# A two-layer encoder trunk on one core: thirteen instead of ten of the second layer's channel-mix double units as seven half-size products, and a higher pace for the sums of weights

## The chip, the cores and the metric

The kernel runs on one NeuronCore of a Trainium2 chip. The metric is the device time of one execution in microseconds (us). A profiled execution adds a trace of every engine: TensorE (PE, with its weight loads shown apart as PEld), VectorE (DVE), ScalarE (ACT), GpSimd (POOL) and SyncE (SP), which here only issues transfers.

## What is computed

The reference is a trunk of two layers over 512 frames of 1024 channels, in float32. Each layer has an mLSTM branch, a retention branch, a merge, a channel mix and a per-layer embedding. The change touches the weights of the channel mix alone:

```python
h2 = rmsnorm(x, norm2_g[i])
x = x + jnp.square(jax.nn.relu(h2 @ w_ff1[i] + b_ff1[i])) @ w_ff2[i] + b_ff2[i]
```

`w_ff1` is 1024 x 4096 and `w_ff2` is 4096 x 1024. "The first product" is the one with `w_ff1`.

## The kernel before

**Units.** Activations lie transposed, channels on the 128 partitions and the 512 frames along a row. A float32 product is made of three matmuls on a value's rounded part (`h`) and its remainder (`l`): `h*h`, `l*h` and `h*l` (lines 480 to 482, 531 to 533 and 575 to 577 of the kernel). All work on TensorE is a list of units (`unit_list`), 275 of them, and the weights of each are loaded by SP, rounded by ScalarE (line 303, tiles `wh_...`) and reduced to their remainder by VectorE (line 304, tiles `wl_...`). Four raw buffers (`wr`) and three pairs of rounded ones stand ahead of TensorE.

**A plain unit (T8)** makes 128 output channels: 8 blocks of 128 input channels times 3 matmuls, each 128 x 128 by 512 frames, 24 matmuls. **A double unit** makes 256 output channels, either as two T8 (48 matmuls of 512 frames) or as a **PAIR**: seven products of half-size blocks in the manner of Strassen and Winograd, named P1 to P7, each of 4 blocks times 3 matmuls over 256 frames (84 matmuls of 256 frames). `run_pair` issues P1, P5, then what the unit before has left over (`flush`), then P6, P2, P3 and P7. Its own P4 is left over, and comes after P5 of the next unit. P1, P6, P7 and P4 follow each other in one PSUM bank (`a`), so P6 can't add to it before P1 has been copied out:

```python
def evict(x, o):
    if x == "P1":
        ac.activation(y[0][:, b], o, AF.Copy)
    elif x == "P5":
        ac.activation(y[1][:, a], o, AF.Copy)
...
        ve.tensor_tensor(y[0][:, b], o, y[0][:, b], OP.add)
```

P1, P5, P6 and P4 are copied out by ScalarE (lines 602, 604, 608 and 614), P2, P3 and P7 added by VectorE (606, 610 and 612).

**Weights of a PAIR.** Seven operands are needed: four given quarters of the weights, of which three are used as they are, and four sums of quarters (`t1` to `t4`). They come in four pieces: A, B and C of 128 x 1024 and D of 128 x 512. For a double unit of the second layer's first product all four sums are made ahead in DRAM, by transfers that add at their destination. GpSimd issues them (line 361, tiles `s...t`). `step` issues one, and `tick` counts a credit that lets the next one go: each unit adds `SHARE` (until the first layer's last gate unit) or `LATER` (after it) times the unit's time less its load, and each sum takes `STEP`. A sum's issue waits for the matmul that stands last at that point. A load of a summed operand waits for its sum.

**The channel mix.** `FPAIRS` names, for each layer, the double units (b, p) of the first product that are a PAIR, where b is one of four blocks of 1024 hidden channels and p one of four double units in it. They are called f02 for (0, 2) and so on below, with layer 1 in the trace's names (`l1f02a`: layer 1 counted from 0, PSUM bank a). The sixteen double units of the second product (o00 to o33) are all PAIRs. The order is f00 to f03, f10, o00 to o03, f11, f12, f13, f20, o10 to o13, f21, f22, f23, f30, o20 to o23, f31 to f33, o30 to o33.

**What follows a unit f (`ff1`).** Each has a tile `st` of 128 x 2048, which holds its 256 x 512 results (as four quarters) and four sums of them. There are two such tiles, taken in turn:

```python
st = cur["ff"].tile([P, 8 * S], F32, name=nm + "st", tag="st", bufs=2)
```

In a PAIR the evictions write into `st` at once, from P1 on. In a unit of two T8, `st` is first written when a T8 has ended. Then come, for each half d: the factor of the norm on VectorE (line 1485), relu and square on ScalarE (1486 and 1487). The second half of channels (d = 1) doesn't need P4, the first one does. Then `pair_quarters` rounds three quarters (`l1hh` by ScalarE, `l1hl` by VectorE, 128 x 768), and `pair_operand` makes four sums (lines 621, 622 and 623 on VectorE) and rounds these (128 x 1024). Only then is the tile `st` free for the unit after the next.

Each engine takes its instructions in one fixed order, which a scheduler writes when the program is built. It puts evictions ahead of what is not due yet.

Of the kernel before, what the change touches and what calls it, by code (L numbers as in the profile page):

```python
# [86 lines left out]

FPAIRS = (((1, 1), (1, 3), (2, 1), (2, 3), (3, 1)), ((0, 2), (1, 0), (1, 1), (1, 3), (2, 0), (2, 1), (2, 3), (3, 0), (3, 1), (3, 2)))  # L90


PRODUCTS = {"P1": ("A", 0, 0), "P5": ("A", 1, 4), "P2": ("B", 0, 2), "P6": ("B", 1, 5), "P3": ("C", 0, 6),
# [14 lines left out]
HALVES = [(WIDE[x][0], u) for x, u in TURNS]  # L108

SOON = ("w_in", 0, CGM + 2 * P)  # L110
STEP, SHARE, LATER = 1.13, 0.75, 0.75
TIME = {"PAIR": (9.9, 3.9), "WIDE": (5.45, 2.7), "FULL": (9.9, 5.0)}


# [32 lines left out]
def groups():  # L147
# [3 lines left out]
    for i in range(L):  # L151
# [11 lines left out]
        for b in range(4):  # L163
            f = [p for c, p in FPAIRS[i] if c == b]
            if f:
# [5 lines left out]
def unit_list(i):  # L171
# [10 lines left out]
    def pair(g, p):  # L182
        u.append(("PAIR", (i, g), p))
# [51 lines left out]
    def pairs(seq):  # L235
        for kind, b, p in seq:
            if (b, p) in FPAIRS[i] and kind == "f":
                pair(f"fp{b}", [q for c, q in FPAIRS[i] if c == b].index(p))
            elif kind == "f":
# [13 lines left out]
def build(ctx, tc, ins, out):  # L253
# [721 lines left out]
    for i in range(L):  # L975
# [501 lines left out]
        def ff1(b, p):  # L1477
# [10 lines left out]

            if (b, p) in FPAIRS[i]:
                def consume(y):  # L1490
                    for d in range(2):
                        evac(d, y[d], SIGN[d])
                    pair_quarters(st, *hid[b, p])
                    pair_operand(nm, st, *hid[b, p])
# [306 lines left out]
```

## Time and profile before

| | |
|---|---|
| three runs | 2314.02, 2317.37 and 2317.66 us, median 2317.37 |
| the profiled execution's own time | 2315.14 us |
| its span, first to last instruction | 2313.4 us |
| PE busy | 2299.1 us (99%) |
| DVE busy | 1766.8 us (76%) |
| ACT busy | 1269.6 us (55%) |
| POOL busy | 624.1 us (27%) |
| granted TensorE clock, mean | 0.998 |
| moved by DMA | 499.36 MB, mean 216 GB/s |

The times of a trace count from the span's start. A row of the timeline has the start, the duration, the engine, the line, the operation, `out<-in`, and in brackets how long the engine had been idle and for whom. The records of two instructions that follow each other without a pause overlap somewhat, so the cost of one in a chain is the distance of two starts. The channel mix of the second layer lies between 1915 and 2250 us.

### The profile page before, as it was taken

The numbers are of one execution on the slowest core, as the hardware profiler recorded it, in microseconds if no ns is written. First come the engines' busy times: TensorE is split into PE (matmuls) and PEld (weight loads), VectorE is DVE, ScalarE is ACT, GpSimd is POOL, SyncE is SP. The second block draws the span as 40 slices with busy tenths as digits, with TensorE's granted clock in tenths as the row PEclk, the third lists the DMA queues.
The fourth block names the chain that finished last, engine by engine and source line by source line (L and its number), as shares of the span: only waits on it lengthen the run. The fifth ranks groups of instructions, "written<-read, shape, count | busy, mean of one in ns | idle before, by whom it ended". The sixth has DMA issues, their size and how long they took to land.

```text
span 2313.4 us, 36468 instructions
## 1 busy us (share of the span) xinstructions
PE 2299.1 (99%) x13532; PEld 2035.4 (88%) x13532; DVE 1766.8 (76%) x2690; ACT 1269.6 (55%) x1837; POOL 624.1 (27%) x984
## 2 busy tenths in 40 slices
PE   9999999999999999999999999999999999999998
PEld 8888899888898899999888888988888888999997
DVE  7878767886676878788778777778867678787785
ACT  6756544644554546556557564445445446566564
POOL 4333222223124322223442332221231242111112
PEclk9999999999999999999999999999999999999999
DMA  7776787777789888888886768877877898878851
GB/s 218 189 191 174 238 228 216 215 227 210 232 230 261 220 228 223 240 239 215 222 224 182 196 174 247 232 216 216 223 221 208 241 266 218 247 232 228 232 160 55
DMA packets 187603, 499.36 MB, mean 216 GB/s; under 512 B 26064, under 2 KB 29520, under 8 KB 187424
## 3 DMA queue, kind: packets, MB, share of 16 engines
q0 software_dynamic: 57520, 188.53, 37.1%
q1 hardware_dynamic: 114496, 281.06, 36.6%
q10 hardware_dynamic: 15408, 27.43, 3.5%
q8 instruction: 106, 1.74, 0.3%
q14 instruction: 73, 0.60, 0.1%
HBM read 478.05 MB, written 194.51 MB: 291 GB/s over the span
## 4 chain that ended last, share of the span: by engine, by line
PE 92%; DVE 5%; ACT 1%; issue 1%; DMA 1%; POOL 0%; SPq 0%; ACTq 0%; DVEq 0%; POOLq 0%
PE l0br L480 1%; PE l1br L480 1%; PE l1br L481 1%; PE l0br L482 1%; PE l1br L482 1%; PE l0br L481 1%; PE l0f L480 1%; PE l0f L481 1%; PE l0f L482 1%; PE l1f L480 1%; PE l1f L481 1%; PE l1f L482 1%; PE l0pg L480 1%; PE l1bm L480 1%; PE l0pg L482 1%
## 5 line engine op out<-in xcount | busy, mean ns | idle before, releaser
L303 ACT ACTIVATE wh<-wr 128x1024 fp32r<-128x1024 f32 (+1 forms) x193 | 199.7, 1041 | 140.5 <-issue 17.1
L304 DVE TENSOR_TENSOR wl<-wr,wh 128x1024 fp32r<-128x1024 f32 (+1 forms) x191 | 234.6, 1230 | 37.5 <-ACT wh L303 36.9
L303 ACT ACTIVATE wh_B<-wr 128x1024 fp32r<-128x1024 f32 x123 | 130.3, 1059 | 184.5 <-PE l0br L481 15.7
L304 DVE TENSOR_TENSOR wl_B<-wr,wh_B 128x1024 fp32r<-128x1024 f32 x123 | 150.3, 1222 | 55.1 <-ACT wh_B L303 50.6
L303 ACT ACTIVATE wh_C<-wr 128x1024 fp32r<-128x1024 f32 x75 | 79.2, 1056 | 69.5 <-PE l0br L481 8.3
L304 DVE TENSOR_TENSOR wl_C<-wr,wh_C 128x1024 fp32r<-128x1024 f32 x75 | 91.7, 1223 | 21.3 <-ACT wh_C L303 17.1
L303 ACT ACTIVATE wh_A<-wr 128x1024 fp32r<-128x1024 f32 x75 | 78.9, 1052 | 44.3 <-DMA wr<-wpairs 5.2
L304 DVE TENSOR_TENSOR wl_A<-wr,wh_A 128x1024 fp32r<-128x1024 f32 x75 | 91.6, 1221 | 12.6 <-ACT wh_A L303 9.4
L303 ACT ACTIVATE wh_D<-wr 128x512 fp32r<-128x512 f32 x75 | 47.2, 630 | 96.5 <-DVE wr L462 27.3
L303 ACT ACTIVATE wh_t<-wr 128x1024 fp32r<-128x1024 f32 x56 | 59.4, 1061 | 69.0 <-PE l0g2va L576 6.0
L304 DVE TENSOR_TENSOR wl_t<-wr,wh_t 128x1024 fp32r<-128x1024 f32 x56 | 68.2, 1221 | 26.1 <-ACT wh_t L303 25.5
L304 DVE TENSOR_TENSOR wl_D<-wr,wh_D 128x512 fp32r<-128x512 f32 x75 | 51.8, 690 | 30.2 <-ACT wh_D L303 28.7
L480 PE MATMUL l0f<-l0n2h,wh 128*128 128x512 f32 x176 | 68.7, 390 | 0.0
L481 PE MATMUL l0f<-l0n2l,wh 128*128 128x512 f32 x176 | 68.6, 390 | 0.0
L482 PE MATMUL l0f<-l0n2h,wl 128*128 128x512 f32 x176 | 68.5, 389 | 0.0
L361 POOL DMA_DIRECT2D s30t<-wpairs x24 | 16.8, 699 | 92.4 <-PE l1o11a L533 9.4
L482 PEld LDWEIGHTS l0f<-l0n2h,wl 128*128 128x128 f32 x176 | 33.0, 188 | 7.0
L480 PEld LDWEIGHTS l0f<-l0n2h,wh 128*128 128x128 f32 x176 | 33.1, 188 | 6.6
L481 PEld LDWEIGHTS l0f<-l0n2l,wh 128*128 128x128 f32 x176 | 33.1, 188 | 6.5
L480 PE MATMUL l1f<-l1n2h,wh 128*128 128x512 f32 x96 | 37.6, 391 | 0.0
L481 PE MATMUL l1f<-l1n2l,wh 128*128 128x512 f32 x96 | 37.5, 390 | 0.0
L482 PE MATMUL l1f<-l1n2h,wl 128*128 128x512 f32 x96 | 37.4, 389 | 0.0
(5797 smaller groups left out, 9132.4 us busy)
## 6 DMA issues: line engine op xcount, KB each, us to landing
wr<-wstream SPq DMA_DIRECT2D x189, 512.0 KB, 4.8
wr<-wpairs SPq DMA_DIRECT2D x225, 256.0 KB, 4.1
wr<-wwide SPq DMA_DIRECT2D x48, 512.0 KB, 4.7
s3t<-wwide POOLq DMA_DIRECT2D x24, 256.0 KB, 5.0
s6t<-wwide POOLq DMA_DIRECT2D x24, 256.0 KB, 5.0
s18t<-wwide POOLq DMA_DIRECT2D x24, 256.0 KB, 4.7
s21t<-wwide POOLq DMA_DIRECT2D x24, 256.0 KB, 5.3
s24t<-wpairs POOLq DMA_DIRECT2D x24, 256.0 KB, 5.7
```

The costliest lines, as they stand in the source:

```text
L303: a = ac.activation(hi_ap, src, AF.Copy)
L304: return a, ve.tensor_sub(lo_ap, src, hi_ap.bitcast(F32))
L361: dma = gp.dma_start(piece(g, x, p, q), piece(g, MADE[x][a], p, q), max_dma_last_dim=4096, **kw)
L480: te.matmul(o, sh, mh, start=first, stop=False)
L481: te.matmul(o, sh, ml, start=False, stop=False)
L482: cur["mm"] = te.matmul(o, sl, mh, start=False, stop=last)
```

## The change

Two constants change. The second layer's tuple of `FPAIRS` gains (0, 3), (1, 2) and (2, 2), and `LATER` goes from 0.75 to 0.79:

```diff
-FPAIRS = (((1, 1), (1, 3), (2, 1), (2, 3), (3, 1)), ((0, 2), (1, 0), (1, 1), (1, 3), (2, 0), (2, 1), (2, 3), (3, 0), (3, 1), (3, 2)))
+FPAIRS = (((1, 1), (1, 3), (2, 1), (2, 3), (3, 1)), ((0, 2), (0, 3), (1, 0), (1, 1), (1, 2), (1, 3), (2, 0), (2, 1), (2, 2), (2, 3), (3, 0), (3, 1), (3, 2)))
...
-STEP, SHARE, LATER = 1.13, 0.75, 0.75
+STEP, SHARE, LATER = 1.13, 0.75, 0.79
```

So f03, f12 and f22 become PAIRs: 6 T8 units go and 3 PAIRs come (272 units instead of 275). Sums of weights rise from 670 to 694 transfers, and the loads by SP by 15. The order of all engines around the three units is written anew. Three places matter.

**ScalarE, from f13's rest to f20's evictions.** Before, where f12 is two T8 (`wh_B`, `wh_D`, `wh_A` are the weights of this and the next unit):

```order
L608 ACTIVATE l1f13st<-l1f13a 128x256
L303 ACTIVATE wh_C<-wr_20741 128x1024
L303 ACTIVATE l1hh_20628<-l1f12st 128x1024
L303 ACTIVATE wh_B<-wr_20763 128x1024
L602 ACTIVATE l1f20st<-l1f20a 128x256
L604 ACTIVATE l1f20st<-l1f20c 128x256
L1486 ACTIVATE l1f13st<-l1f13st,bc 128x512
L1487 ACTIVATE l1f13st<-l1f13st 128x512
L614 ACTIVATE l1f13st<-l1f13a 128x256
```

The same stretch after the change:

```order
L303 ACTIVATE wh_B<-wr_20897 128x1024
L1486 ACTIVATE l1f13st<-l1f13st,bc 128x512
L614 ACTIVATE l1f13st<-l1f13a 128x256
L303 ACTIVATE l1hh_20732<-l1f12st 128x1024
L303 ACTIVATE wh_D<-wr_20945 128x512
L1486 ACTIVATE l1f13st<-l1f13st,bc 128x512
L1487 ACTIVATE l1f13st<-l1f13st 128x512
L602 ACTIVATE l1f20st<-l1f20a 128x256
L604 ACTIVATE l1f20st<-l1f20c 128x256
```

The copy of f20's P1 (line 602) stood ahead of f13's relu, and now stands behind both of them, behind f13's P4 and behind the last rounding of f12's tile `st`, which f20 takes over. The place of f22, f23 and f30 reads the same with other names.

**VectorE in the same stretch, after the change** (`wl_C` and `wl_B` are weights of f20):

```order
L610 TENSOR_TENSOR l1f13st<-l1f13c,l1f13st 128x256
L304 TENSOR_TENSOR wl_C<-wr_20875,wh_C 128x1024
L612 TENSOR_TENSOR l1f13st<-l1f13a,l1f13st 128x256
L304 TENSOR_TENSOR l1hl_20733<-l1f12st,l1hh_20732 128x768
L621 TENSOR_TENSOR l1f12st<-l1f12st 128x512
L304 TENSOR_TENSOR wl_B<-wr_20897,wh_B 128x1024
L622 SCALAR_TENSOR_TENSOR l1f12st<-l1f12st 128x256
L1485 TENSOR_TENSOR l1f13st<-l1f13st,l1n2rb 128x512
L623 SCALAR_TENSOR_TENSOR l1f12st<-l1f12st 128x256
L1485 TENSOR_TENSOR l1f13st<-l1f13st,l1n2rb 128x512
L304 TENSOR_TENSOR l1hl_20733<-l1f12st,l1hh_20732 128x1024
```

Before, the rows between f13's P3 and the factor of its norm were these:

```order
L610 TENSOR_TENSOR l1f13st<-l1f13c,l1f13st 128x256
L304 TENSOR_TENSOR l1hl_20629<-l1f12st,l1hh_20628 128x1024
L612 TENSOR_TENSOR l1f13st<-l1f13a,l1f13st 128x256
L304 TENSOR_TENSOR wl_B<-wr_20763,wh_B 128x1024
L1485 TENSOR_TENSOR l1f13st<-l1f13st,l1n2rb 128x512 x2
```

So the last rounding of f12's `st` stood right behind f13's P3, and now stands behind f13's P7, behind two roundings of weights and behind both halves of f13's norm.

**TensorE at f10, where P2 (bank b) and P6 (bank a, with `wh_B`) meet.** Before, P6 ends and P2 begins:

```order
L531 MATMUL l1f10a<-l1nsh_19086,wh_B 128x256
L532 MATMUL l1f10a<-l1nsl_19094,wh_B 128x256
L533 MATMUL l1f10a<-l1nsh_19086,wl_B 128x256
L531 MATMUL l1f10b<-l1n2h_19062,wh_B 128x256
L532 MATMUL l1f10b<-l1n2l_19063,wh_B 128x256
```

After the change P2 ends, three matmuls of the next unit o00 follow, and then P6 begins:

```order
L532 MATMUL l1f10b<-l1n2l_19117,wh_B 128x256
L533 MATMUL l1f10b<-l1n2h_19116,wl_B 128x256
L531 MATMUL l1o00a<-l1hh_19513,wh_A 128x256
L532 MATMUL l1o00a<-l1hl_19514,wh_A 128x256
L531 MATMUL l1o00c<-l1hh_19513,wh_A 128x256
L531 MATMUL l1f10a<-l1nsh_19122,wh_B 128x256
```

P2 is put ahead of P6 in f20 and f30 too, without matmuls of another unit between them. On ScalarE, `wh_A` of o00 stands right ahead of the copy of f10's P1, as the last of six instructions behind the first relu of f03: that relu, the 128 x 1024 rounding of f02, the copy of f03's P4, `wh_D`, a square of f03, `wh_A`. On VectorE the rows from f03's P3 to the factor of its norm are those shown for f13, except that `wl_C` stands ahead of P3 and the 128 x 768 rounding ahead of P7.

## Prediction

> **What bounds the kernel now.** I read the page first: how busy each engine is, and whose work the chain that ended last consists of.
>
> ```profile
> PE 2299.1 (99%) x13532; PEld 2035.4 (88%) x13532; DVE 1766.8 (76%) x2690; ACT 1269.6 (55%) x1837; POOL 624.1 (27%) x984
> PE 92%; DVE 5%; ACT 1%; issue 1%; DMA 1%; POOL 0%; SPq 0%; ACTq 0%; DVEq 0%; POOLq 0%
> ```
>
> TensorE is busy for 99% of the span and makes up 92% of the chain. So time taken off TensorE goes off the end, as long as nothing makes TensorE wait. Whether something does is read from the stage of the change, the second layer's channel mix. I asked for busy time there by stretches (columns: length, then PE, PEld, DVE, ACT and POOL busy with counts, then clock, DMA share, GB/s), and for the two PAIRs f13 and f20, which follow each other there already.
>
> ```profile
> 1930.00:2000.00 70.00, 69.93 (x516) 66.30 (x515) 57.76 (x85) 46.10 (x62) 13.54 (x21) 1.00 0.84 237
> 2000.00:2070.00 70.00, 70.00 (x546) 67.82 (x545) 55.78 (x84) 44.57 (x62) 10.47 (x18) 1.00 0.83 238
> 2070.00:2140.00 70.00, 70.00 (x545) 67.96 (x544) 52.58 (x78) 42.92 (x61) 10.95 (x17) 1.00 0.82 230
> ...
> 2029.63:2039.71 10.08, 10.08 (x86) 10.07 (x85) 10.05 (x15) 8.47 (x12) 2.09 (x3) 1.00 0.83 242
> 2039.71:2049.79 10.08, 10.08 (x87) 10.08 (x86) 7.62 (x11) 8.04 (x13) 1.30 (x2) 1.00 0.87 226
> ```
>
> TensorE is idle for 0.07 of these 210 us. But over f13 VectorE works 10.05 of 10.08 us and ScalarE 8.47. A PAIR of the first product is a heavy load for the engines that serve TensorE, and over the stretches of 70 us, which hold plain units and o units too, VectorE has only 12 to 17 us left. The change makes runs of such PAIRs longer: f02, f03, f10, and f11, f12, f13, f20, and f21, f22, f23, f30.
>
> **What it takes off TensorE.** Three rows of the timeline bound f12, now two T8, and one product of f13.
>
> ```profile
> 2017.27 0.40 PE L480 MATMUL l1f<-l1n2h,wh 128*128 128x512 f32 x1
> ...
> 2029.63 0.28 PE L531 MATMUL l1f13a<-l1n2h,wh_A 128*128 128x256 f32 x1
> ...
> 2031.07 0.28 PE L531 MATMUL l1f13c<-l1nsh,wh_A 128*128 128x256 f32 x1
> ```
>
> A product of 12 matmuls takes 2031.07 - 2029.63 = 1.44 us, so a PAIR takes 7 x 1.44 = 10.08 us. From f12's first matmul to f13's first are 12.36 us, in which f11's P4 (1.44) is done too, so f12's two T8 take 10.92 us. Each replaced unit saves 0.84 us, three save **2.5 us**. By the Trainium skill (TensorE: Matmul & The Clock Gate, "Wait — 56ns, not 53.3ns?") matmuls on a warm clock start N / 2.4 GHz + 2.5 ns apart: 109.2 ns at 256 columns and 215.7 ns at 512. By it a unit would save 48 x 0.2157 - 84 x 0.1092 = 1.18 us, an estimate, and the sum below would be 1.0 us lower. The rows above show 120 ns at 256 columns, and they decide.
>
> **What it adds on ScalarE and VectorE, and who waits.** f20 takes over the tile `st` of f12. Its P1 can be copied out only when f12's last rounding has read `st`, and its P6 can add to the bank only after that copy. Now f12's results are there early, since a T8 is evicted at its end. As a PAIR, f12 gets its P4 only in the midst of f13, and its rest slides to f20. The durations are read from VectorE and ScalarE over f20 and the start of o10 in the profile of before, where nearly the same instructions follow each other:
>
> ```profile
> 2043.31 0.69 DVE L1485 TENSOR_TENSOR l1f13st<-l1f13st,l1n2rb 128x512 f32<-128x512 f32 x1 [1.99 <-ACT l1f13st L614]
> ...
> 2048.11 0.95 DVE L304 TENSOR_TENSOR l1hl<-l1f13st,l1hh 128x768 fp32r<-128x768 f32 x1
> 2048.98 0.42 DVE L612 TENSOR_TENSOR l1f20st<-l1f20a,l1f20st 128x256 f32<-128x256 f32 x1
> 2049.31 0.68 DVE L621 TENSOR_TENSOR l1f13st<-l1f13st 128x512 f32<-128x512 f32 x1
> 2049.91 1.22 DVE L304 TENSOR_TENSOR wl_B<-wr,wh_B 128x1024 fp32r<-128x1024 f32 x1
> 2051.05 0.42 DVE L622 SCALAR_TENSOR_TENSOR l1f13st<-l1f13st 128x256 f32<-128x256 f32 x1
> 2051.38 0.42 DVE L1523 TENSOR_TENSOR l1x<-l1x,l1o10a 128x256 f32<-128x256 f32 x1
> ```
>
> ```profile
> 2041.35 0.39 ACT L604 ACTIVATE l1f20st<-l1f20c 128x256 f32<-128x256 f32 x1 [1.05 <-PE l1f20c L533]
> 2041.63 0.71 ACT L1486 ACTIVATE l1f13st<-l1f13st,bc 128x512 f32<-128x512 f32 x1
> 2042.37 0.63 ACT L1487 ACTIVATE l1f13st<-l1f13st 128x512 f32<-128x512 f32 x1
> 2042.91 0.36 ACT L614 ACTIVATE l1f13st<-l1f13a 128x256 f32<-128x256 f32 x1
> 2043.17 0.62 ACT L303 ACTIVATE wh_D<-wr 128x512 fp32r<-128x512 f32 x1
> 2043.70 1.05 ACT L303 ACTIVATE wh_A<-wr 128x1024 fp32r<-128x1024 f32 x1
> 2044.64 0.37 ACT L608 ACTIVATE l1f20st<-l1f20a 128x256 f32<-128x256 f32 x1
> 2044.91 0.72 ACT L1486 ACTIVATE l1f13st<-l1f13st,bc 128x512 f32<-128x512 f32 x1
> 2045.55 1.06 ACT L303 ACTIVATE wh_C<-wr 128x1024 fp32r<-128x1024 f32 x1
> ```
>
> Read as distances of starts, VectorE needs 0.87 for the 128 x 768 rounding, 0.33 for an eviction (line 612) and for line 622, 0.60 for line 621 and 1.14 for 128 x 1024 of weights. Line 1485 takes 0.69 to its end. ScalarE needs 0.64 for line 1486, 0.54 for 1487, 0.26 for 614, 0.53 for `wh_D`, 0.94 for 128 x 1024, and 0.39 to the end of a copy like line 604. A hand-over is 0.04 us: line 614 ends at 2043.27, and VectorE, which waited for it, starts at 2043.31.
>
> *f20.* Count from TensorE's start of f13. Seven products are 10.08 us, so f20 starts at 10.08, and its order is P1, P5, f13's P4, P2, P6: P6 is due at 10.08 + 4 x 1.44 = **15.84**. f13's P3 is its sixth product (after P1, P5, f12's P4 and two more) and gives way to the next at 8.64. Its last matmul began 0.12 before and takes 0.28, so VectorE evicts it (610) from 8.84. Behind that stand, in the new order, `wl_C`, 612, the 768 rounding, 621, `wl_B`, 622 and the first 1485: 0.33 + 1.14 + 0.33 + 0.87 + 0.60 + 1.14 + 0.33 + 0.69 = 5.43, to 14.27. ScalarE waits for this with line 1486, and behind it stand 614, the 128 x 1024 rounding of f12, `wh_D`, 1486, 1487 and only then f20's P1: 0.64 + 0.26 + 0.94 + 0.53 + 0.64 + 0.54 + 0.39 = 3.94, from 14.31 to 18.25. TensorE can start P6 at 18.3, **2.5 us late**. What VectorE does in between for f12 (second 1485, its last rounding) fits beside these 3.94 us: 0.60 + 1.14 after line 614 has ended.
>
> *f30.* The rows are the same, and so is the price: **2.5 us**.
>
> *o00.* Here f03 and f10 take the parts of f13 and f20, but the first to be late are o00's early matmuls, due at the same 15.84, which need `wh_A`. VectorE: from 8.84, 0.33 + 0.87, then P7's eviction not before 10.08 + 0.20 = 10.28, then 0.33 + 0.60 + 1.14 + 0.33 + 0.69, to 13.37. ScalarE from 13.41: 0.64 + 0.94 + 0.26 + 0.53 + 0.54 and 1.05 to the end of `wh_A`, to 17.37: 1.6 us late. `wl_C` stands right ahead of P3's eviction here and may hold it up by half a microsecond or so, so 1.6 to 2.2, and I take **1.9 us**.
>
> Everything not named here is taken to be on time, so with these durations the three are lower ends. They could be longer by a few tenths each, as a weight load that now can't overlap comes after each wait.
>
> **What else moves.** The sums and loads:
>
> ```profile
> q0 software_dynamic: 57520, 188.53, 37.1%
> wr<-wpairs SPq DMA_DIRECT2D x225, 256.0 KB, 4.1
> ```
>
> To 670 sums come 24 more, and behind the first layer's last gates a T8 gives a credit of 0.79 x 5.45 - 1.5 = 2.81 instead of 2.59, so sums come 8% faster and end earlier. Queue q0 takes 37.1% of the DMA engines, so its part rises by some 3 points, and the DMA share of 0.82 to 0.84 above leaves room. The loads of a PAIR are seven of 256 KB instead of two of 512 KB, 0.75 MB more, in all 2.25 MB, which at 237 GB/s is 9.5 us of DMA work spread over three places of some 40 us. I cost both at nothing, hidden by TensorE's work on the units between load and use. If the cover is gone somewhere, a load comes late by up to its own landing, 4.1 us. Below nothing: the sums end earlier, but since TensorE waits for no load now, nothing is to be gained.
>
> **The sum.** -2.5 + 1.9 + 2.5 + 2.5 = **+4.4 us**. The profiled execution took 2315.14 us, so 2319.5 in its terms; the median of the runs, 2317.37, lies 2.2 above it, so **2321.8 us**.
>
> **Rivals.** *The waits don't come* (not slower). From P3's eviction to the end of P1's copy the chain for f20 takes 5.43 + 0.04 + 3.94 = 9.4 us, and it decides from 15.84 - 8.84 = 7.0 us on. If its instructions ran together more closely than in the rows above and it stayed below that, nothing would wait. For it speaks that TensorE waits for neither of f13 and f20 now, though they are neighbours already. Against it: f20's copy stood ahead of f13's relu there, and an engine takes its rows in turn. Then only -2.5 is left: 2317.37 - 2.5 = 2314.9. If half of each wait remains, 2318.3.
>
> *Loads come late as well.* For it: a DMA share of 0.83 in this stage and more sums in all of the second layer. Against it: each landed in time before. One late load of 4.1 us makes 2325.9.
>
> *The clock drops in a wait.* The end of the kernel, where TensorE idles most, shows the only lower clock:
>
> ```profile
> 2260.00:2313.40 53.40, 43.73 (x289) 39.82 (x288) 32.04 (x65) 22.97 (x49) 11.79 (x16) 0.93 0.16 50
> ```
>
> There 9.7 us of idleness go with a clock of 0.93 over 53.4 us, worth at most 3.7 us. A like loss after one of the new waits would make 2325.5. The same page of the Trainium skill (Part 1, "The HAM clock gate") has the clock halved after an idle window of about 3.4 us. By that rule waits of 2.5 us leave it alone, and no run here shows a wait like them.
>
> *The change doesn't act:* the new order shows the three PAIRs, so this is left out.
>
> **How the numbers follow.** All three waits with -2.5 beside them: 65%, from 2319.5 to 2324. Waits partly or wholly hidden: 20%, 2314.9 to 2319. Late loads or a lower clock: 15%, 2325 to 2329. The range from 2315.5 to 2327 leaves out the ends. A bound of 0.2% is 4.6 us, about what a measurement of this kernel can tell from no change, and the forecast of +4.4 lies almost on it. Terms left out (weight loads after a wait, late loads) only add. So slower by more than that: half of the first case, and all of the third, 0.50. Within it 0.46, as the second case is there too, and faster 0.04.
>
> **What would show it.** In the changed kernel TensorE should be idle for 1.6 to 2.2 us at o00's first matmuls and 2.5 us at P6 of f20 and of f30, for ScalarE. f12 should take 10.08 us. ScalarE should wait for VectorE's line 1485 just ahead. No idle time of TensorE there, or one that a transfer ends, would prove me wrong.

## The result, and the profile after

The changed kernel takes 2327.14 us (median of four runs, 2324.94 to 2329.61), the kernel before, on the same chip, 2316.41 (four runs). The ratio is 1.0044, with a 95% interval of 1.0032 to 1.0057: **10.2 us slower, 7.4 to 13.2**. (The ratio is estimated from all runs; the medians alone lie 10.7 apart.) I had forecast 2321.8, 4.4 us slower, so the sign was right and the size less than half of what came, and the median stands at the upper end of the range, 2327. Everything below is about the two parts: the three waits that were forecast, and what came on top.

The two lines of the page of the changed kernel that answer to those of before, busy time and the chain:

```profile
PE 2302.0 (99%) x13640; PEld 2042.4 (88%) x13640; DVE 1776.3 (76%) x2705; ACT 1275.0 (55%) x1855; POOL 643.3 (28%) x1008
PE 85%; DVE 8%; DMA 2%; ACT 2%; issue 2%; POOL 0%; DVEq 0%; ACTq 0%; SPq 0%; POOLq 0%
```

TensorE's 99% hardly tells anything: its share of the chain fell from 92 to 85%, and that is the work of other engines now standing on the path. The waits of TensorE in the changed kernel (us in total, times, longest) name the places, and the same three stretches as before (the last three columns are the granted clock, the DMA share and GB/s) give their weight:

```profile
PE l1f30a L531 <- ACT l1f30st L602: 2.4, 1, 2.4
PE l1f20a L531 <- ACT l1f20st L602: 2.3, 1, 2.3
PE l1o00a L531 <- ACT wh_A L303: 2.2, 1, 2.2
```

```profile
1930.00:2000.00 70.00, 67.84 (x503) 64.68 (x503) 59.49 (x92) 46.56 (x68) 14.64 (x22) 1.00 0.80 230
2000.00:2070.00 70.00, 67.71 (x554) 67.34 (x553) 54.32 (x80) 42.64 (x64) 10.67 (x17) 0.98 0.81 233
2070.00:2140.00 70.00, 67.75 (x568) 67.42 (x567) 54.50 (x81) 40.30 (x58) 6.77 (x10) 1.00 0.76 227
```

TensorE is idle for 2.2 to 2.3 us in each stretch, where it had 0.07 in all three together. The middle one also shows a clock of 0.98. Now the chain behind f20, counted in the prediction from f13's start, here at 2037.31. VectorE and ScalarE of the changed kernel:

```profile
2046.40 0.42 DVE L610 TENSOR_TENSOR l1f13st<-l1f13c,l1f13st 128x256 f32<-128x256 f32 x1 [0.17 <-PE l1f13c L533]
2046.74 1.22 DVE L304 TENSOR_TENSOR wl_C<-wr,wh_C 128x1024 fp32r<-128x1024 f32 x1
...
2050.81 0.42 DVE L622 SCALAR_TENSOR_TENSOR l1f12st<-l1f12st 128x256 f32<-128x256 f32 x1
2051.14 0.68 DVE L1485 TENSOR_TENSOR l1f13st<-l1f13st,l1n2rb 128x512 f32<-128x512 f32 x1
```

```profile
2051.86 0.73 ACT L1486 ACTIVATE l1f13st<-l1f13st,bc 128x512 f32<-128x512 f32 x1 [3.05 <-DVE l1f13st L1485]
2052.49 0.36 ACT L614 ACTIVATE l1f13st<-l1f13a 128x256 f32<-128x256 f32 x1
2052.76 1.05 ACT L303 ACTIVATE l1hh<-l1f12st 128x1024 fp32r<-128x1024 f32 x1
2053.71 0.62 ACT L303 ACTIVATE wh_D<-wr 128x512 fp32r<-128x512 f32 x1
2054.23 0.71 ACT L1486 ACTIVATE l1f13st<-l1f13st,bc 128x512 f32<-128x512 f32 x1
2054.84 0.62 ACT L1487 ACTIVATE l1f13st<-l1f13st 128x512 f32<-128x512 f32 x1
2055.36 0.37 ACT L602 ACTIVATE l1f20st<-l1f20a 128x256 f32<-128x256 f32 x1
```

P1's copy ends at 2055.73, 18.42 after f13's start; 18.25 was forecast. The difference arose at the head: the eviction of P3 began 0.25 later than counted. From there to the end of the copy it took 9.33 us, where the rows of before gave 9.41. TensorE's last matmul before P6 and P6's first, in the changed kernel:

```profile
2053.21 0.28 PE L533 MATMUL l1f20b<-l1n2h,wl_B 128*128 128x256 f32 x1
2055.78 0.39 PE L531 MATMUL l1f20a<-l1nsh,wh_B 128*128 128x256 f32 x1 [2.29 <-ACT l1f20st L602]
...
2056.97 0.41 PE L533 MATMUL l1f20a<-l1nsh,wl_B 128*128 128x256 f32 x1
2057.18 0.41 PE L531 MATMUL l1f20a<-l1nsh,wh_B 128*128 128x256 f32 x1
```

The first two starts lie 2.57 apart where 0.12 would do: 2.45 us lost. And 0.8 us behind the wait the matmuls go from 0.12 apart to 0.21, as the last two rows show. That is the clock, which the experiments come back to.

**Where the time is.** Two distances on TensorE tell stages apart: f02's first matmul, and from there to the first matmul of the last norm (`l1n41ss`). Each row is one execution; the two of the changed kernel (changed and after2) differ by 1.2 us in the first distance and 0.4 in the second. Ratios are estimated from all runs, against the kernel before on the same chip, and differ from the ratio of the medians by up to 0.0006.

| kernel | PAIRs, LATER | ratio (95%) | f02 starts | f02 to last norm |
|---|---|---|---|---|
| before | 10, 0.75 | 1 | 1938.5 | 364.1 |
| changed | 13, 0.79 | 1.0044 (1.0032 to 1.0057) | 1946.2 | 371.0 |
| after2 | 13, 0.79 | 1.0046 (1.0034 to 1.0059) | 1945.0 | 371.4 |
| pace_alone | 10, 0.79 | 1.0012 (1.0003 to 1.0021) | 1944.4 | 362.5 |
| three_tiles | 13, 0.79 | 1.0015 (1.0006 to 1.0024) | 1941.6 | 365.6 |
| pace_0775 | 13, 0.775 | 1.0044 (1.0031 to 1.0056) | 1944.2 | 370.5 |
| pace_085 | 10, 0.85 | 1.0035 (1.0023 to 1.0047) | 1946.8 | 364.6 |
| tile_ten | 10, 0.75 | 0.9998 (0.9989 to 1.0007) | 1941.1 | 364.7 |
| only_12 | 11, 0.79 | 1.0018 (1.0009 to 1.0027) | 1939.2 | 368.9 |
| f01_split | 11, 0.755 | 1.0003 (0.9995 to 1.0012) | 1937.7 | 367.8 (f01's P4 falls in it) |
| late_pace | 13, 0.75 and 0.85 | 1.0039 (1.0027 to 1.0052) | 1940.1 | 370.3 |
| late_three_tiles | 13, 0.75 and 0.85 | 1.0004 (0.9995 to 1.0013) | 1944.7 | 364.2 |
| ten_late | 10, 0.70 and 0.95 | 1.0030 (1.0018 to 1.0042) | 1944.1 | 367.9 |

In the stage of the change the changed kernel loses 371.0 - 364.1 = 6.9 us. This is steady: the four kernels with thirteen PAIRs and the old tile (changed, after2, pace_0775, late_pace) take 370.3 to 371.4, those with ten and a `LATER` of 0.75 to 0.85 throughout 362.5 to 364.7. The rest of the 10.2, some 3 us, is lost ahead of it, where no unit of TensorE was changed. The profiled execution of the changed kernel was the slowest of its four (2329.61), that of before faster than its median (2315.14), so f02 lies as much as 7.7 us apart there. Nor is all of that waiting. TensorE's busy time ahead of f02 in before, in pace_alone (told below) and in the changed kernel (the first two numbers of a row behind its window are the length and PE's busy time):

```profile
0.00:1938.47 1938.47, 1934.01 (x10788) 1686.42 (x10789) 1479.43 (x2253) 1049.61 (x1520) 564.36 (x902) 1.00 0.79 220
0.00:1944.38 1944.38, 1936.71 (x10788) 1689.05 (x10789) 1479.53 (x2253) 1050.22 (x1520) 595.26 (x946) 1.00 0.81 225
0.00:1946.22 1946.22, 1936.45 (x10788) 1687.37 (x10789) 1479.26 (x2253) 1049.94 (x1520) 596.74 (x946) 1.00 0.81 225
```

It is idle for 4.5, 7.7 and 9.8 us. So of the 7.7 us by which f02 comes later in the changed kernel 5.3 are waits; for the other 2.4 TensorE is busy longer with the same 10788 matmuls, and in pace_alone for 2.7 of 5.9.

### The profile page after: what moved, and what is told of

Same layout as the page of the kernel before. It is cut to its first block, busy times and chain, and to the rows that moved or that the text cites. A ratio compares the mean times of both kernels' runs of the same rounds, so it can differ in the third digit from the quotient of the medians.

```text
span 2327.9 us, 36799 instructions
## 1 busy us (share of the span) xinstructions
PE 2302.0 (99%) x13640; PEld 2042.4 (88%) x13640; DVE 1776.3 (76%) x2705; ACT 1275.0 (55%) x1855; POOL 643.3 (28%) x1008
## 4 chain that ended last, share of the span: by engine, by line
PE 85%; DVE 8%; DMA 2%; ACT 2%; issue 2%; POOL 0%; DVEq 0%; ACTq 0%; SPq 0%; POOLq 0%
PE l0br L480 1%; PE l1br L480 1%; PE l1br L482 1%; PE l0br L481 1%; PE l0br L482 1%; PE l1br L481 1%; PE l0f L480 1%; PE l0f L481 1%; PE l0f L482 1%; DVE wl_B L304 1%; DMA wr<-wpairs 1%; PE l0pg L480 1%; PE l0bm L480 1%; PE l0pg L482 1%; PE l1bm L481 1%
## 5 line engine op out<-in xcount | busy, mean ns | idle before, releaser
L303 ACT ACTIVATE wh<-wr 128x1024 fp32r<-128x1024 f32 (+1 forms) x187 | 193.5, 1041 | 140.1 <-issue 17.1
L304 DVE TENSOR_TENSOR wl<-wr,wh 128x1024 fp32r<-128x1024 f32 (+1 forms) x185 | 227.1, 1229 | 34.9 <-ACT wh L303 34.3
L695 POOL TENSOR_TENSOR l1n3sum<-l1n3sum,l1n3sq 128x512 f32<-128x512 f32 x6 | 8.2, 1369 | 155.1 <-ACT l1n3sum L687 132.6
L361 POOL DMA_DIRECT2D s27t<-wpairs x24 | 17.3, 730 | 63.6 <-PE l1g2va L577 17.0
L361 POOL DMA_DIRECT2D s6t<-wwide x24 | 17.3, 720 | 61.7 <-PE l0g0va L577 20.4
```

The costliest lines, as they stand in the source:

```text
L303: a = ac.activation(hi_ap, src, AF.Copy)
L304: return a, ve.tensor_sub(lo_ap, src, hi_ap.bitcast(F32))
L361: dma = gp.dma_start(piece(g, x, p, q), piece(g, MADE[x][a], p, q), max_dma_last_dim=4096, **kw)
L695: (add or gp).tensor_tensor(self.sum, self.sum, sq, OP.add)
```

## The experiments

Theory A is that of the prediction, with what the first trace added: the three waits stand on the reuse of `st`, and the higher pace of the sums costs something earlier. The rivals B to E are told in the expectations.

**after2**, the changed kernel once more.

> The changed kernel once more, beside the kernel before and the three below. In its first profile the span was 14.5 us longer than before; 7.8 us of that had arisen before the second layer's channel mix, behind loads of weights that landed late. Theory A (the three waits on ScalarE, and the higher pace of the sums, which makes loads late in the stretch from 600 to 1900 us): the time is again 9 to 12 us above before, TensorE waits again 2.2 to 2.4 us for ScalarE at o00, f20 and f30, and 5 to 8 us are lost ahead of 1900 us. Rival B (the late loads were bad luck of one execution): the three waits are there, but ahead of 1900 us 2 us or less are lost, and the time is 4 to 6 us above before.

Measured: 10.7 us above before (7.9 to 13.7), waits of 2.5, 2.3 and 2.4 us, and f02 again 6.5 us late. Neither the waits nor the size of the loss was an accident of one execution. Theory A held here, B fell.

**pace_alone** takes the three PAIRs back and keeps LATER at 0.79:

```diff
-FPAIRS = (..., ((0, 2), (0, 3), (1, 0), (1, 1), (1, 2), (1, 3), (2, 0), (2, 1), (2, 2), (2, 3), (3, 0), (3, 1), (3, 2)))
+FPAIRS = (..., ((0, 2), (1, 0), (1, 1), (1, 3), (2, 0), (2, 1), (2, 3), (3, 0), (3, 1), (3, 2)))
```

> Only LATER goes from 0.75 to 0.79; the PAIRs stay the ten of before. Theory A (the pace makes loads late): 5 to 8 us slower than before, about 2322 to 2324, lost between 600 and 1900 us, with VectorE's line 459 or ScalarE's line 303 waiting for loads of weights there. Rival B (chance): within 2 us of before, about 2316 to 2318, and PE not behind at 1900 us.

Measured: 2.8 us slower than before (0.7 to 4.9). So the pace has a price of its own, about half of what A asked, and in the trace nothing of it lies in the stage of the change (362.5 us there). Rival B's 2 us lie within the interval, but f02 is 5.9 us late, which B excluded. VectorE waits longer for raw weights ahead of 1930 us; the rows (total, times, longest) of before, of pace_alone and of pace_085, in this order:

```profile
DVE wr L459 <- DMA wr<-wpairs: 11.0, 10, 2.8
```

```profile
DVE wr L459 <- DMA wr<-wpairs: 15.7, 9, 3.7
```

```profile
DVE wr L459 <- DMA wr<-wpairs: 21.8, 11, 4.6
```

The pace alone doesn't set this row, though: it reads 13.9 us in tile_ten and 16.5 in late_pace (told further down), which run at 0.75 ahead of 1640 us, and 11.9 in only_12 at 0.79.

**three_tiles** takes away what makes P1's copy wait: another tile to write to, in the same memory.

```diff
-st = cur["ff"].tile([P, 8 * S], F32, name=nm + "st", tag="st", bufs=2)
+if i:
+    st = cur["ff"].tile([P, 4 * S], F32, name=nm + "st", tag="st", bufs=3)
+    sm = cur["ff"].tile([P, 4 * S], F32, name=nm + "sm", tag="sm", bufs=1)
...
-pair_operand(nm, st, *hid[b, p])
+pair_operand(nm, st, sm, *hid[b, p])
```

> The changed kernel with the second layer's tile st split in the same memory: the results of a unit (128 x 1024) go through three tiles, its four sums (128 x 1024) have one tile of their own. So a unit's P1 no longer waits for the last rounding of the unit before the last. Theory A: the waits of 2.2 to 2.4 us at o00, f20 and f30 go, so the time falls by 6 to 9 us below the changed kernel (7 us of waits, and 1.6 us of halved clock if that follows a wait), to 2 to 5 us above before. Rival C (VectorE and ScalarE have too much to do over the runs of PAIRs, and the tile is only where it shows): the waits move to other places, as the roundings or the evictions come late themselves, and the time stays within 3 us of the changed kernel.

Measured: 2320.40 beside 2328.74 for after2 on the same chip, 8.3 us less by the medians and 7.2 by the ratios. ScalarE of three_tiles around the same copy (line 1486 is 1492 here):

```profile
2043.79 0.39 ACT L602 ACTIVATE l1f20st<-l1f20a 128x256 f32<-128x256 f32 x1 [0.35 <-PE l1f20a L533]
2045.23 0.39 ACT L604 ACTIVATE l1f20st<-l1f20c 128x256 f32<-128x256 f32 x1 [1.05 <-PE l1f20c L533]
2046.17 0.73 ACT L1492 ACTIVATE l1f13st<-l1f13st,bc 128x512 f32<-128x512 f32 x1 [0.56 <-DVE l1f13st L1491]
```

The copy stands ahead of f13's relu again and waits for TensorE alone. All three waits are gone: shown, their cause is the reuse of the tile. In the traces the stage is 5.8 us shorter than in after2, and f02 comes 3.3 us earlier, where the split tile has no part. Rival C has a grain of truth. What TensorE waits for in three_tiles from 1930 us on is small and new:

```profile
PE l1o20a L531 <- DVE l1x L1529: 0.5, 1, 0.5
PE l1o10a L531 <- DVE l1x L1529: 0.4, 1, 0.4
PE l1o00a L531 <- ACT l1hh L303: 0.4, 1, 0.4
```

With the four of 0.3 us behind these rows that is 2.5 us, as much as the three units save. It can be why the stage, 365.6 us, doesn't come below 364.1.

**pace_0775** (LATER 0.775 instead of 0.79 in the changed kernel).

> The changed kernel with LATER 0.775 instead of 0.79, the lowest pace tried here at which all sums of the thirteen PAIRs come ahead of their loads. Theory A with a cost that goes with the pace: the loss ahead of 1900 us falls from 5 to 8 us to 3 to 5, and the time to 2 to 3 us below the changed kernel; the three waits of 2.2 to 2.4 us stay. If single collisions of a load with sums decide, their place changes and the loss may go up or down by 3 us. Rival B: no difference (within 1 us).

Measured: 10.2 us above before (7.2 to 13.0), and beside after2 0.8 above by the medians and 0.5 below by the ratios. The gain of 2 to 3 us that a cost in proportion to the pace asked doesn't show; what came is rival B's no difference, as far as intervals of some 3 us each way can tell. The waits stay at 1.8, 2.3 and 2.3 us.

**pace_085** (the ten PAIRs, LATER 0.85).

> The ten PAIRs of before with LATER 0.85, two and a half times the step to 0.79, which alone cost 2.8 us (0.7 to 4.9). Theory A (the pace makes loads late): the cost grows with the step, 5 to 9 us above before, all of it ahead of the second layer's channel mix. Rival D (a few loads happen to meet sums in another order, and the pace as such costs nothing): between 2 us below and 4 us above before.

Measured: 8.1 us above before (5.3 to 10.9), f02 at 1946.8, the stage 364.6. In a large step the pace does cost, all of it ahead of the channel mix. D fell.

**tile_ten** (the split tile in the kernel before).

> The kernel before (ten PAIRs, LATER 0.75) with the second layer's tile st split as in three_tiles. TensorE didn't wait for the copy of a P1 before, so by theory A the split alone is worth nothing: within 2 us of before. If it were worth 4 us or more, the gain of three_tiles would not be from the three new waits.

Measured: 0.9998 (within 2.5 us of before). The split is worth nothing by itself, so what three_tiles gains in the stage is the three waits and what hung on them.

**only_12**: `FPAIRS` with (1, 2) alone added, LATER 0.79.

> Only (1, 2) is added to the ten PAIRs, with LATER 0.79, so beside pace_alone one T8 pair becomes a PAIR. Theory A: TensorE waits at P6 of f20 for 2.3 to 2.5 us and at no other place, so 2.4 - 0.84 = 1.6 us above pace_alone, and 3.2 if the clock is halved after it. The clock by the windows seen so far (3.41 us each, counted from its first record): halved if 2.2 us or more of the wait lie in one window, not if less than 1.7. Rival C (VectorE and ScalarE are behind by then because of the run f02, f03, f10, which here isn't made longer): the wait at f20 is shorter by 1 us or more.

Measured: 4.2 us above before (2.1 to 6.3), 1.4 more than pace_alone by the ratios. TensorE waits 2.3 us at P6 of f20, as long as in the changed kernel, so C fell; a wait of 0.8 us for ScalarE at f10, which A had not named, is there too. The clock was halved, as the rule of windows said; then A asked for 3.2 us more than pace_alone, and with intervals of some 2 us each way 1.4 can't be told from that. In its trace the stage is 4.8 us longer than before, and f02 comes only 0.7 us later, at the same pace as in pace_alone: the price of the pace doesn't show in every execution.

**f01_split**: another choice of PAIR, f01 in place of the three, with the split tile and LATER 0.755.

> Another choice: eleven PAIRs, the ten of before and (0, 1), with the split tile of three_tiles and LATER 0.755. Here f01 and f02 stand side by side and a unit of two T8 follows, so no run of four PAIRs arises. Theory A: no wait of TensorE over 0.3 us is new, and the unit saves 0.84 us: 0 to 2 us below before. Rival C: waits of 0.4 to 0.6 us at the o units behind, as in three_tiles, and the time is 0 to 2 us above before.

Measured: 1.0003, no change. Four waits of 0.2 us at o00, o01 and o10 are new, which add up to about the 0.84 us. The waits are as small as A said, the time is nearer to C's, and the interval of 2 us each way leaves it open.

**late_pace**: the changed kernel with the old pace up to the second layer's last gate unit.

```diff
-STEP, SHARE, LATER = 1.13, 0.75, 0.79
+STEP, SHARE, LATER, LATEST = 1.13, 0.75, 0.75, 0.85
...
+late_from = units.index(("WIDE", (1, "rw2"), 0))
...
-at["credit"] += (SHARE if at["unit"] <= rush else LATER) * t - load
+at["credit"] += (SHARE if at["unit"] <= rush else LATER if at["unit"] <= late_from else LATEST) * t - load
```

> The thirteen PAIRs, but the sums go at 0.75 as before until the second layer's last gate unit (about 1640 us) and at 0.85 only from there, where so far no load came late. Theory A (the higher pace costs about 3 us between 300 and 1650 us): 2.5 to 3.5 us below the changed kernel, 6.5 to 8 above before; the waits of TensorE over 0.4 us ahead of f02, which add up to 2.8 and 5.2 us in two kernels at 0.75 and to 6.4 to 9.1 us at 0.79 with thirteen PAIRs, come to 3 to 5.5; the three waits on ScalarE stay. Rival E (the sums crowd behind 1640 us and make loads late there): the time is that of the changed kernel within 1.5 us, with new waits between 1640 and 2000 us.

Measured: 9.0 us above before (6.3 to 12.0), 1 to 2 us below the changed kernel where 2.5 to 3.5 were expected, and the intervals overlap: undecided. The profiled execution, in which f02 starts 6 us earlier than in the changed kernel, was the fastest of its five (2322.62, median 2326.36). In its trace TensorE's waits over 0.4 us ahead of f02 come to about 5 us, as A asked. But the trace speaks against a part of A. One load that is late in the changed kernel is late here too, though by then as many sums have been issued as before (473 by 1473 us). VectorE's line 459 (460 in late_pace) at that load, in before, the changed kernel and late_pace:

```profile
1461.80 0.69 DVE L459 TENSOR_TENSOR wr<-wr,wr 128x512 f32<-128x512 f32 x1 [0.72 <-DMA wr<-wpairs]
```

```profile
1470.43 0.69 DVE L459 TENSOR_TENSOR wr<-wr,wr 128x512 f32<-128x512 f32 x1 [3.74 <-DMA wr<-wpairs]
```

```profile
1464.22 0.69 DVE L460 TENSOR_TENSOR wr<-wr,wr 128x512 f32<-128x512 f32 x1 [2.87 <-DMA wr<-wpairs]
```

**late_three_tiles**: both edits, the split tile and the late pace.

> Both repairs: the split tile of three_tiles and the pace of late_pace. Theory A: three_tiles was 2.2 times a thousandth less 0.7 above before, or 3.5 us, and 3 us of it are the pace, so within 1.5 us of before. Small waits of 0.4 to 0.6 us at o00, o10 and o20 stay, which take up what the three PAIRs save. Rival E: 2 us or more above before.

Measured: 0.9 us above before (-1.2 to 3.0), where three_tiles was 3.5 above (1.4 to 5.6). Expected within 1.5: held by the ratio, though the medians lie 1.7 us apart and the interval reaches into rival E's 2 us. That the late pace brought the difference isn't shown: the intervals overlap, and f02 starts at 1944.7 in its profiled execution, the slowest of eleven, as late as in pace_alone. In time this version can't be told from the kernel before, and no version tried beats that kernel.

**late_shift**: late_pace with twelve more matmuls in o02, ahead of f20.

```diff
-for k in range(4):
+for k in [0, 1, 2, 3] * (2 if (name, x) == ("l1o02", "P5") else 1):
```

> late_pace with 12 more matmuls: product P5 of o02 is done twice, of which the second result counts, so that the waits of f20 and f30 come 1.41 us later and as long. It asks only for the clock: by the rule of windows (3.41 us each from the clock's first record on) the clock is halved behind a wait of which 2.2 us or more lie in one window, and not behind one with 1.7 or less there; which waits those are is to be read from the trace, in late_pace too. If it is instead always f20's wait that halves it, the rule is wrong and the cause lies in what stands there.

This one is about the clock. Its records start at 5.23, 5.90, 6.06 and 3.99 us in the four kernels below, and every change lies a whole number of windows of 3.413 us later (in the changed kernel the first one at 2056.64, 601 windows on). 1.00 is the full clock and 0.50 the half one. With the time cut at these windows (columns as in the stretches above: length, PE busy with its matmuls, and at the end the clock), first the changed kernel at f20, then late_pace at f20, then late_shift at f20, then late_three_tiles at an early unit of the first layer, where TensorE happened to wait 2.0 us for an eviction:

```profile
2053.23:2056.64 3.41, 1.12 (x10) 0.92 (x9) 2.69 (x5) 3.41 (x8) 0.00 (x0) 1.00 0.32 111
2056.64:2060.06 3.42, 3.42 (x18) 3.42 (x18) 3.02 (x4) 2.82 (x4) 0.00 (x0) 0.50 0.37 95
2060.06:2063.47 3.41, 3.41 (x31) 3.41 (x31) 2.46 (x6) 2.07 (x3) 0.50 (x1) 1.00 0.41 148
```

```profile
2043.66:2047.07 3.41, 3.16 (x27) 2.95 (x25) 2.53 (x5) 1.87 (x4) 0.81 (x1) 1.00 0.93 273
2047.07:2050.48 3.41, 1.37 (x11) 1.37 (x12) 2.85 (x4) 3.41 (x8) 0.00 (x0) 1.00 0.72 174
2050.48:2053.90 3.42, 3.42 (x18) 3.42 (x17) 2.93 (x6) 2.38 (x4) 0.00 (x0) 0.50 0.39 110
```

```profile
2047.24:2050.65 3.41, 1.56 (x13) 1.35 (x12) 2.43 (x4) 3.41 (x6) 0.00 (x0) 1.00 0.92 184
2050.65:2054.06 3.41, 2.97 (x25) 2.98 (x25) 2.91 (x5) 3.37 (x8) 0.00 (x0) 1.00 0.62 160
```

```profile
318.02:321.43 3.41, 1.36 (x12) 1.16 (x11) 3.03 (x5) 0.38 (x1) 0.81 (x2) 1.00 0.81 219
321.43:324.85 3.42, 3.42 (x19) 3.42 (x18) 2.11 (x4) 1.48 (x3) 0.50 (x1) 0.50 0.53 170
```

Where PE is busy for 1.37 us or less of a window here, the next window runs at half the clock: 18 or 19 matmuls instead of 31, so some 13 x 0.12 = 1.5 us lost. Where it is busy for 1.56 or more, the clock stays. f20's wait is as long in late_shift as in the others (2.3 us), but the window's edge cuts it, and the clock stays: it isn't f20 that does it, but where the wait lies. The windows at the waits of after2, pace_0775 and only_12 agree (1.28, 1.13 and 1.12 busy, halved), and so do those of o00 and f30 in all runs (1.71 or more, not halved). The border holds for these streams of matmuls only. At the kernel's end, where the stream stops and matmuls of 2 columns follow with pauses, the clock is halved behind windows of which PE is busy for longer, as in f01_split:

```profile
2303.18:2306.60 3.42, 1.99 (x16) 1.71 (x15) 2.21 (x8) 1.81 (x7) 0.72 (x1) 1.00 0.27 90
2306.60:2310.01 3.41, 2.19 (x8) 1.72 (x8) 1.81 (x5) 0.61 (x3) 1.08 (x2) 0.50 0.00 0
```

late_shift ran once, at 2323.55 us.

**ten_late**: the ten PAIRs with a lower early pace (LATER 0.70, LATEST 0.95 in the lines of late_pace).

> The ten PAIRs of before, with the sums at 0.70 instead of 0.75 until the second layer's last gate unit and at 0.95 from there. Theory A (waits for loads ahead of f02 grow with the pace): 1 to 3 us below before, with waits over 0.4 us ahead of f02 that add up to 3 us or less. Rival D (below 0.75 the pace no longer decides): within 1 us of before.

Measured: 7.0 us slower than before (4.2 to 9.7). Theory A is refuted in this direction, and D too. The run changes two paces at once, a lower one early and a higher one late, so it doesn't show what the lower one costs by itself. In the stage, 3.8 us longer than before, ScalarE waits for loads of summed weights, as the sums come late (from 1930 us on; the tensors `s..t` hold sums):

```profile
ACT wh_B L303 <- DMA wr<-s26t: 6.1, 3, 2.8
ACT wh_B L303 <- DMA wr<-s27t: 4.7, 2, 2.4
ACT wh_A L303 <- DMA wr<-s25t: 2.4, 1, 2.4
```

With the smaller rows behind these they come to 18.7 us. In the kernel before the same answer has two such waits, 3.6 us in all.

## Why the prediction was right and where it fell short

**Right: the order that sets the waits.** ScalarE's new order puts the copy of f20's P1 behind f13's relu, and that relu waits 3.05 us for line 1485, as forecast. Both waits at P6 were priced at 2.5 us; they came to 2.45 and 2.6 by the starts of the matmuls. A little luck is in that: at f20 the copy ended 0.17 us later than counted, and TensorE came to P6 0.18 later too. three_tiles took the waits away with the tile alone. The rival that no wait comes is refuted: the instructions ran no closer together than in the rows of before.

**Right: the saving.** f12's first matmul is at 2027.23 and f13's at 2037.31: 10.08 us, as worked out. The matmuls of the new PAIR start 120 ns apart. The rule of N / 2.4 GHz + 2.5 ns in the Trainium skill (TensorE: Matmul & The Clock Gate, "Wait — 56ns, not 53.3ns?") gives 109 ns, by which the prediction estimated a saving of 1.18 us for a unit; in this stage the measured 120 decides.

**Too small: o00's term, 1.9 us.** It measured 2.3 (starts of 1970.57 and 1973.02, less 0.12) and 2.7 in after2. The rounding `wl_C` stands ahead of P3's eviction there. I gave it half a microsecond; VectorE's rows show that it held P3 from 1963.69, when it was due, to 1964.72, so 1.0 us, of which a quarter went into the pause that I had counted ahead of P7's eviction:

```profile
1963.58 1.23 DVE L304 TENSOR_TENSOR wl_C<-wr,wh_C 128x1024 fp32r<-128x1024 f32 x1 [0.27 <-ACT wh_C L303]
1964.72 0.42 DVE L610 TENSOR_TENSOR l1f03st<-l1f03c,l1f03st 128x256 f32<-128x256 f32 x1
```

**Wrong: "by that rule waits of 2.5 us leave it alone".** That was said of the clock, and the rival went into a 15% case. The Trainium skill (TensorE: Matmul & The Clock Gate, Part 1 "The HAM clock gate") has the clock halved after an idle window of about 3.4 us that doesn't start with the kernel. The windows are there, of 3.413 us. But here they needn't be idle throughout: a wait of 2.0 to 2.5 us inside one was enough, six times out of six. In the four traces with all three waits and thirteen unchanged PAIRs (changed, after2, pace_0775 and late_pace) one of the three hit each time, at 1.5 us. The sum had nothing for it; the rival had priced it at 3.7 us.

In the stage the terms now read -2.5 + 2.3 + 2.45 + 2.6 + 1.5 = +6.4, and measured is +6.9. o02 and o03, which took 9.52 us each before and 9.89 here (as below), add 0.7, and the other units together take a little off again.

**Wrong: "I cost both at nothing", the sums and the loads.** Ahead of the channel mix some 3 us are lost. pace_alone measured 2.8, and pace_085 8.1. "Each landed in time before" was a reading of TensorE's waits alone: ahead of 1930 us VectorE waited 11.0 us for raw weights in ten waits, so there was less cover than that. And what came isn't one load that is late by 4.1 us: TensorE's longest new waits ahead of f02 in the changed kernel are 1.4, 1.3 and 1.2 us, at three places, and a part of the delay isn't waiting at all. So "up to its own landing, 4.1 us" was near in size by luck, and putting late loads at 15% was the error. That loads land a little later at many places, and that a part of it reaches TensorE where VectorE has no slack, fits the rows and isn't shown. How the pace does it stays open: late_pace has a late load with the sums of before, only_12 hardly any delay at f02 with the higher pace, and ten_late, lower early and higher late, costs more.

The chances were added up loosely too: half of 65% and all of 15% is 0.475, not 0.50.

So of the 10.2 us, 6.9 lie in the stage by the traces and come from the tile, the clock and small change; 2.8 (0.7 to 4.9) are shown to come with the pace, without the path from sum to load being settled.

## What to carry to other kernels

When a unit is made faster on the engine that bounds, count forward the chain that frees what the unit after the next writes into, in the order that each in-order engine will have; with the durations of neighbours that chain came out to within 0.2 us. Before dropping such a change, ask whether the buffer that waits needs to be that large: half a tile in three buffers took back 7 to 8 us at no cost in memory. And price a knob that was moved along with the change by itself: here the pace alone cost 2.8 us, about what the three units save.

## What the runs showed of the hardware

The clock's half rate hangs on where a wait lies, not only on its length. Of the waits of 1.9 to 2.7 us, the six that left TensorE busy for at most 1.37 us of one 3.413 us window were followed by one window at 0.5, and those with 1.56 or more were not. What decides between 1.37 and 1.56 no run shows, and at the kernel's end, with matmuls of 2 columns among them, a window with 1.99 us of busy time was followed by the half clock too. So the busy time of this view isn't the whole rule.

The same products of a PAIR ran at two speeds. In o02 of the kernel before and of the changed kernel the first matmul and the first of the next unit are:

```profile
1988.17 0.28 PE L531 MATMUL l1o02a<-l1hh,wh_A 128*128 128x256 f32 x1
...
1997.69 0.28 PE L531 MATMUL l1o03a<-l1hh,wh_A 128*128 128x256 f32 x1
```

```profile
1997.39 0.28 PE L531 MATMUL l1o02a<-l1hh,wh_A 128*128 128x256 f32 x1
...
2007.29 0.28 PE L531 MATMUL l1o03a<-l1hh,wh_A 128*128 128x256 f32 x1
```

That is 9.52 and 9.90 us for 84 matmuls, 113 and 118 ns each, with nobody waiting. In before and in pace_alone the faster speed begins behind a pause in o01 (starts 0.35 and 0.42 us apart) and holds to the end of o03; in the changed kernel a pause of 0.22 there changes nothing. The same unit has the one speed in some kernels and the other in others (o02 takes 9.52 in pace_alone and 9.89 in pace_085, which differ in the pace alone). What chooses it is open; over a dozen units 0.37 us each would be worth 4.4 us, as much as separates two executions here.
